# Transposing small tiles on VectorE instead of TensorE, and a new order for short matrix products in a hybrid attention trunk

## The chip, the cores and the metric

The kernel runs on one core of a Trainium2 chip. The metric is device time in microseconds for one execution of the whole program. One execution was also recorded by the hardware profiler. All stretches, rows and waits below come from that record.

The engines have short names in the profile: PE is TensorE (matrix products), PEld its loads of the stationary operand, DVE is VectorE, ACT is ScalarE, POOL is GpSimd, and SP issues most DMAs. L180 means line 180 of the kernel before.

## What is computed

The reference is a two-layer trunk over 512 tokens of width 1024, with 16 learned "meta" tokens prepended. Each layer normalises the residual, projects it, runs two causal mixers side by side (a pooling mixer and a latent attention with 8 heads) and adds the gated sum back. Cut to what matters here:

```python
kv = (c_kv @ w_kv_b).reshape(B, L, N_HEADS, QK_NOPE_DIM + V_HEAD_DIM)
k_nope, v = kv[..., :QK_NOPE_DIM], kv[..., QK_NOPE_DIM:]
...
q = rmsnorm(q, g_qn)
k = rmsnorm(k, g_kn)
...
s = jnp.einsum('bqhd,bkhd->bhqk', q[:, q0:kend], k[:, :kend]).astype(jnp.float32) * scale
s = jnp.where(valid, s, MASK_VALUE)
p = jax.nn.softmax(s, axis=-1).astype(v.dtype)
outs.append(jnp.einsum('bhqk,bkhd->bqhd', p, v[:, :kend]))
...
h_res = h_res + merged @ w_out[l]
```

Every ordinary token attends to the 16 meta tokens and to the ordinary tokens before it. Each meta token attends to the meta tokens before it. The meta tokens' own outputs are needed after layer 0 but not after layer 1.

## The kernel before

**Precision by splitting.** Each float32 operand is split into a high part in the fast matrix format (`fp32r`) and the low rest. ScalarE makes the high part by a copy, VectorE the low part by a subtraction. The helper `split` does this for a tile. A product then takes three passes, high x high, high x low and low x high (`mm3`, L180 to L182).

**Stream and order.** All projections of both layers form one list (`plan`), run by the generator `stream` in steps of a few passes. The layer's other work is written by hand in `Layer.go` and pulls the stream forward with `step`, `fill`, `fill_now` and `upto`, so that projection passes stand between the parts of the attention. `after` defers a piece by an amount of stream time; `LAG` is 2000 ns. The written order is a priority: a scheduler then places every instruction on its engine's queue by a simulated time line, taking the first in the written order whose operands are ready there. `behind(a, b)` makes `a` wait for `b`.

**Attention.** `head` handles one head: score products into PSUM tiles named S, masking and row extremum on VectorE (`top`), exponentials on ScalarE (`expo`), normalisation on POOL (L818 for the 16 meta columns, L820 for the rest). Query tile i holds 128 queries, and its keys are the meta tokens and the 128(i+1) tokens up to its end. The score product of query tile 0 has 144 columns.

The probabilities of the head before (`prev`) are multiplied with the values in `pv`. For every key tile j, TensorE transposes the 4-j probability tiles (L839), `split` takes them out of PSUM as `th` and `tl`, and two products add to the output tile `o`: one with a stationary of 128 columns (high and low values side by side, L844), and one with a stationary of 64 columns (L845) for the low probabilities. `pv(prev, (0, 1))` does key tiles 0 and 1, `pv(prev, (2, 3))` the other two. `go` calls the second one after the next head's `prep`.

**Meta tokens.** The 16 meta columns of the probabilities of two heads are collected in `pm`, 128 x 4 x 32 numbers. At the odd head, `pv` splits `pm` into `pmr` (L833, L834), transposes it by four products with an identity (`identr`, L850), and copies the result out of PSUM into `mt`, as high, low and high again (L853, L854). One product of `mt` with the block-diagonal meta values `vb` then adds the meta part for both heads (L868). `vb` is made in `v_body`: six passes of 512 columns with the meta tokens' latent replicated eight times as stationary (tile name `pa`), then a mask and copies that move rows between partitions (L673 to L675).

**Small sums.** The squared norms of queries and keys are summed by products into two PSUM tiles, copied to SBUF by `stat_rows`, transposed in `qk_stats` by five TensorE transposes (L716, L717) and turned into factors by Newton steps on VectorE. In `meta_queries` (layer 0), the meta tokens' own probabilities are transposed by one TensorE transpose (L889) and spread by small copies.

Of the kernel before, what the change touches and what calls it, by code (L numbers as in the profile page):

```python
# [71 lines left out]
def trunk(ctx, tc, xT, xrow, mrow, pos, win, wkr, wqb, wkb, wvb, wgr, wpu, wmu, wout, gains, const, yT):  # L72
# [65 lines left out]
    gp.memset(maskw[:, :512 - P], 0.0)  # L138
    identr = cp.tile([P, P], F32R, name="identr")

    def other_loads(made):
        for k in range(2, 8):
            behind(sp.dma_start(xb[:, k, :T], xT[:, k, :]), made)
            if k in (3, 4):
                raw = rawt()
                behind(sp.dma_start(raw, win[0, MT_CKV + k - 3, :, 512:1024]), made)
                early.append(raw)
        behind(sp.dma_start(cst, const), made)
        behind(sp.dma_start(posb[:, :T], pos.partition_broadcast(P)), made)
        dve.tensor_copy(maskw[:, 512 - P:], cst[:, C_MASK:C_MASK + P])  # L150
        dve.tensor_copy(identr, ident)

# [117 lines left out]
    def split(hi, lo, src, a, b):  # L270
        act.activation(hi[:, a:b], src, AF.Copy)  # L271
        dve.tensor_sub(lo[:, a:b], src, hi[:, a:b].bitcast(F32))  # L272

# [35 lines left out]
    class Layer:  # L309
# [191 lines left out]

        def stat_rows(self, x0):
            t = tmp()
            for s, (a, b) in enumerate(FULL):
                a = max(a, x0)
                g, o_ = 32 * s, HALF * s
                act.activation(t[0:H, a:b], self.st[s][g:g + H, a - o_:b - o_], AF.Copy)
                dve.tensor_add(t[0:H, a:b], self.st[s][g + 64:g + 64 + H, a - o_:b - o_], t[0:H, a:b])
            return t

        def k_sums(self):
            self.stat_go(5)
            sp.dma_start(ksr[self.l], self.stat_rows(0)[0:H, 0:T])

# [122 lines left out]
        def v_body(self, k, w):  # L637
# [18 lines left out]
            for k in range(2):  # L656
                rep = []
                for t in cs[k]:
                    r = slot("pa", F32R, bufs=2, w=416)[:, 0:P].rearrange("p (a b) -> p a b", a=8)
                    dve.tensor_copy(r, t[:, 0:NM].bitcast(F32).unsqueeze(1).to_broadcast([P, 8, NM]))  # L660
# [3 lines left out]
            dve.scalar_tensor_tensor(out=vf[:, :512].rearrange("p (a b) -> p a b", a=8),  # L664
                                     in0=ps.rearrange("p (a b) -> p a b", a=8), scalar=self.ninv[:, 4:5],
                                     in1=cst[:, C_VBD:C_VBD + 8].unsqueeze(2).to_broadcast([P, 8, 64]),
                                     op0=ALU.mult, op1=ALU.mult)
            fh, fl = tmp(), tmp()
            act.activation(fh[:, :512].bitcast(F32R), vf[:, :512], AF.Copy)
            dve.tensor_sub(fl[:, :512].bitcast(F32R), vf[:, :512], fh[:, :512])  # L670
            for p in range(4):
                r, c = slice(32 * p, 32 * p + 32), slice(P * p, P * p + P)
                gp.tensor_copy(self.vb[0:32, c], fh[r, c])  # L673
                act.activation(self.vb[32:64, c], fh[r, c], AF.Copy)
                gp.tensor_copy(self.vb[64:96, c], fl[r, c])  # L675
            yield 6 * 216
# [30 lines left out]
        def qk_stats(self):  # L707
            fill_now(LAG + 100)
            self.stat_go(7)
            sts = self.stat_rows(self.x0)  # L710
            if self.last:
                dve.memset(sts[0:H, 0:NM], 1.0)
            fill_now(2600)
            stp = mmt()
            for j in range(4):
                pe.transpose(stp[:, H * j:H * j + H], sts[0:H, NM + P * j:NM + P * (j + 1)], ident[0:H, 0:H])  # L716
            pe.transpose(stp[0:NM, 4 * H:5 * H], sts[0:H, 0:NM], ident[0:H, 0:H])  # L717
            na, ny, nt = (sm.tile([P, 5, H], F32, tag=t, name=nm(t)) for t in ("na", "ny", "nt"))
            dve.memset(na[:, 4, :], 1.0)
            eps = self.eps.unsqueeze(2).to_broadcast([P, 5, H])  # L720
            for r, j, k in ((P, 0, 4), (NM, 4, 5)):
                dve.scalar_tensor_tensor(out=na[0:r, j:k, :], in0=stp[0:r, H * j:H * k].rearrange("p (a b) -> p a b", b=H),
                                         scalar=1.0 / QK, in1=eps[0:r, j:k, :], op0=ALU.mult, op1=ALU.add)
            newton(ny, na, nt)
            self.nqs = sm.tile([P, 5, H], F32, tag="nqs", name=nm("nqs"))
            dve.tensor_scalar(self.nqs, ny, -1.0 / math.sqrt(QK), None, op0=ALU.mult)
            fill_now(9500)
            if not self.last:
                self.smeta = sm.tile([NM, 8, NM], F32, tag="smeta", name=nm("smeta"))

# [28 lines left out]
        def head(self, h, kq, prev):  # L759
# [62 lines left out]

        def pv(self, prev, js):
            if prev is None:
                return
            h, pt, pm = prev
            p, odd = h // 2, h % 2
            if js[0] == 0:
                self.o = sct() if h == H - 1 else pp.tile([P, 512], F32, tag="o", name=nm("o"), bufs=1)
            ops = self.o  # L830
            if odd == 1 and js[0] == 0:
                self.pmr = sm.tile([P, 4, 2, 32], F32R, tag="pmr", name=nm("pmr"))
                act.activation(self.pmr[:, :, 0, :], pm, AF.Copy)  # L833
                dve.tensor_sub(self.pmr[:, :, 1, :], pm, self.pmr[:, :, 0, :].bitcast(F32))  # L834
            for j in js:
                n = SEQ - P * j
                tr = mmt()
                for i in range(j, 4):
                    pe.transpose(tr[:, P * (i - j):P * (i - j + 1)], pt[i][:, NM + P * j:NM + P * (j + 1)], ident)  # L839
                th = tp.tile([P, W], F32R, tag="th", name=nm("th"), bufs=2)  # L840
                tl = tp.tile([P, W], F32R, tag="tl", name=nm("tl"), bufs=2)
                split(th, tl, tr[:, :n], 0, n)
                out = ops[:, P * j:512]
                pe.matmul(out, vt[:, j, h, :], th[:, :n], start=j == 0, stop=j == 3)  # L844
                pe.matmul(out[0:64], vt[:, j, h, 0:64], tl[:, :n], start=False, stop=j == 3, skip_group_check=True)  # L845
            if js[-1] != 3:
                if odd == 1:
                    tr = sct() if h == H - 1 else mmt()
                    for i in range(4):
                        pe.matmul(tr[0:64, P * i:P * (i + 1)], self.pmr[:, i].rearrange("p a b -> p (a b)"), identr,  # L850
                                  start=True, stop=True)
                    self.mt = slot("racc", F32R)
                    act.activation(self.mt[0:64, 0:512], tr[0:64, :], AF.Copy)  # L853
                    act.activation(self.mt[64:96, 0:512], tr[0:32, :], AF.Copy)  # L854
                return
            if odd == 0:
                self.op = tmp()
# [19 lines left out]
        def meta_queries(self):  # L877
# [9 lines left out]
            dve.tensor_mul(smeta, smeta, bc(mxm))  # L887
            tr = mmt()
            pe.transpose(tr[:, 0:NM], smeta.rearrange("p a b -> p (a b)"), ident[0:NM, 0:NM])  # L889
            mh = sm.tile([96, 4 * NM], F32R, tag="mh", name=nm("mh"))  # L890
            for p in range(4):
                r, c = slice(32 * p, 32 * p + 32), slice(NM * p, NM * p + NM)
                act.activation(mh[0:32, c], tr[r, 0:NM], AF.Copy)
                act.activation(mh[64:96, c], tr[r, 0:NM], AF.Copy)
                dve.tensor_sub(mh[32:64, c], tr[r, 0:NM], mh[0:32, c].bitcast(F32))
            self.mo = sm.tile([P, 4 * NM], F32, tag="mo", name=nm("mo"))
# [120 lines left out]
        def go(self, nxt):  # L1017
# [52 lines left out]
            self.pv(prev, (0, 1))  # L1070
            if not self.last:
                self.meta_queries()
            fill_now(2600)
            self.pv(prev, (2, 3))
            up("gm7")
# [86 lines left out]
```

## Time and profile before

| | |
|---|---|
| time, median of 3 runs | 778.08 us (778.04 to 778.8) |
| time of the profiled execution | 778.45 us |
| its span, first to last instruction | 776.6 us |
| instructions in the span | 14527 |
| granted TensorE clock, mean | 0.999 |

A row of the profile's groups names the line, engine and operation, what is written and read, the shapes, the count, and then the busy time in us and the mean ns of one. Timelines give start and duration in us. A matrix product's duration overlaps the next one's, since TensorE pipelines them; the distance between starts shows the pace. Some records of matrix products are missing from the trace, so counts of neighbours in a timeline can be one short.

### The profile page before, as it was taken

The numbers are of one execution on the slowest core, as the hardware profiler recorded it, in microseconds if no ns is written. First come the engines' busy times: TensorE is split into PE (matmuls) and PEld (weight loads), VectorE is DVE, ScalarE is ACT, GpSimd is POOL, SyncE is SP. The second block draws the span as 40 slices with busy tenths as digits, with TensorE's granted clock in tenths as the row PEclk, the third lists the DMA queues.
The fourth block names the chain that finished last, engine by engine and source line by source line (L and its number), as shares of the span: only waits on it lengthen the run. The fifth ranks groups of instructions, "written<-read, shape, count | busy, mean of one in ns | idle before, by whom it ended". The sixth has DMA issues, their size and how long they took to land.

```text
span 776.6 us, 14527 instructions
## 1 busy us (share of the span) xinstructions
PE 771.7 (99%) x5251; PEld 702.8 (90%) x5251; DVE 534.3 (69%) x1155; ACT 414.2 (53%) x930; POOL 206.9 (27%) x265
## 2 busy tenths in 40 slices
PE   9999999999999999999999999999999999999998
PEld 8999899999999999999997898887788888888887
DVE  5588688357788977785466486774577888765932
ACT  6755656545666665633354365455446666654420
POOL 1026404012334242052120263030132433420500
PEclk9999999999999999999999999999999999999999
DMA  8533234433222222325643332244232332122372
GB/s 284 164 112 98 74 92 123 123 96 103 92 82 87 79 67 71 96 82 153 188 134 91 110 89 87 79 132 141 76 123 89 96 89 89 59 79 68 108 241 85
DMA packets 54932, 84.04 MB, mean 108 GB/s; under 512 B 10007, under 2 KB 18583, under 8 KB 54861
## 3 DMA queue, kind: packets, MB, share of 16 engines
q1 hardware_dynamic: 54716, 82.86, 35.2%
q8 instruction: 41, 0.67, 0.4%
q14 instruction: 31, 0.25, 0.1%
q10 hardware_dynamic: 144, 0.26, 0.1%
HBM read 76.68 MB, written 4.29 MB: 104 GB/s over the span
## 4 chain that ended last, share of the span: by engine, by line
PE 99%; DMA 1%; SPq 0%; ACT 0%; DVE 0%; issue 0%
PE mm L180 29%; PE mm L182 29%; PE mm L181 29%; PE mm L839 2%; PE S L181 2%; PE S L182 2%; PE S L180 2%; PE o L844 1%; PE o L845 1%; PE S L498 1%; DMA raw<-win 1%; PE S L462 0%; PE mm L868 0%; PE mm L387 0%; PE mm L850 0%; PE S L845 0%
## 5 line engine op out<-in xcount | busy, mean ns | idle before, releaser
L180 PE MATMUL mm<-hh,whi 128*128 128x264 f32 (+2 forms) x1096 | 345.4, 317 | 0.3 <-ACT whi L175 0.3
L181 PE MATMUL mm<-hl,whi 128*128 128x264 f32 (+2 forms) x1096 | 343.2, 314 | 0.0
L182 PE MATMUL mm<-hh,wlo 128*128 128x264 f32 (+2 forms) x1096 | 342.5, 314 | 0.0
L176 DVE TENSOR_TENSOR wlo<-raw,whi 128x512 fp32r<-128x512 f32 (+2 forms) x251 | 181.4, 726 | 103.7 <-ACT whi L175 101.4
L175 ACT ACTIVATE whi<-raw 128x512 fp32r<-128x512 f32 (+2 forms) x251 | 150.5, 603 | 178.9 <-PE mm L181 134.3
L180 PEld LDWEIGHTS mm<-hh,whi 128*128 128x128 f32 x1096 | 205.5, 188 | 13.6 <-ACT whi L175 0.5
L181 PEld LDWEIGHTS mm<-hl,whi 128*128 128x128 f32 x1096 | 206.1, 188 | 12.0
L182 PEld LDWEIGHTS mm<-hh,wlo 128*128 128x128 f32 x1096 | 205.2, 188 | 12.2
L743 POOL TENSOR_TENSOR tmp<-kp,bc 64x528 f32<-64x528 f32 x16 | 24.8, 1552 | 103.7 <-issue 53.5
L818 POOL TENSOR_TENSOR pm<-pa,rs 128x16 f32<-128x16 f32 x32 | 11.7, 365 | 148.6 <-DVE rs L813 148.6
L604 POOL TENSOR_TENSOR racc<-racc,tmp 128x264 f32<-128x264 f32 (+1 forms) x15 | 14.3, 957 | 113.9 <-ACT tmp L603 113.9
L928 POOL TENSOR_TENSOR tmp<-tmp,xb 128x264 f32<-128x264 f32 (+1 forms) x24 | 26.7, 1134 | 57.7 <-DVE tmp L926 55.5
L774 DVE CUSTOM_DVE_ANT_0 S<-S,maskw,nqs 128x272 f32<-128x272 f32 (+4 forms) x80 | 38.4, 498 | 2.2 <-PE S L182 1.9
L180 PE MATMUL mm<-u,whi 128*128 128x264 f32 (+1 forms) x108 | 35.1, 325 | 0.0
L182 PE MATMUL mm<-u,wlo 128*128 128x264 f32 (+1 forms) x108 | 34.7, 321 | 0.0
L180 PE MATMUL mm<-cq,whi 128*128 128x264 f32 (+1 forms) x108 | 34.6, 321 | 0.0
L181 PE MATMUL mm<-cq,whi 128*128 128x264 f32 (+1 forms) x108 | 34.6, 321 | 0.0
L182 PE MATMUL mm<-cq,wlo 128*128 128x264 f32 (+1 forms) x108 | 34.6, 320 | 0.0
L272 DVE TENSOR_TENSOR tl<-mm,th 128x512 fp32r<-128x512 f32 (+1 forms) x64 | 29.3, 482 | 7.0 <-ACT th L271 6.0
L781 ACT ACTIVATE cq<-S,bia 128x400 f32<-128x400 f32 (+2 forms) x48 | 24.5, 515 | 17.8 <-DVE bia L808 8.8
L820 POOL TENSOR_TENSOR cq<-cq,rs 128x384 f32<-128x384 f32 (+1 forms) x32 | 33.5, 1047 | 0.0
L271 ACT ACTIVATE th<-mm 128x512 fp32r<-128x512 f32 (+1 forms) x64 | 25.4, 434 | 6.5 <-PE mm L839 5.9
(271 smaller groups left out, 1370.8 us busy)
## 6 DMA issues: line engine op xcount, KB each, us to landing
raw<-win SPq DMA_DIRECT2D x143, 256.0 KB, 2.6
raw<-wout SPq DMA_DIRECT2D x32, 256.0 KB, 3.0
bc<-kdr SPq DMA_DIRECT2D x16, 264.0 KB, 3.1
raw<-wpu SPq DMA_DIRECT2D x16, 256.0 KB, 2.9
raw<-wmu SPq DMA_DIRECT2D x16, 256.0 KB, 2.7
raw<-wqb SPq DMA_DIRECT2D x12, 256.0 KB, 3.0
xb<-xT SPq DMA_DIRECT2D x8, 264.0 KB, 5.5
tmp<-xT SPq DMA_DIRECT2D x16, 132.0 KB, 3.4
```

The source lines that it names most:

```text
L175: act.activation(hi[:, :n], raw[:, :n], AF.Copy)
L176: dve.tensor_sub(lo[:, :n], raw[:, :n], hi[:, :n].bitcast(F32))
L180: pe.matmul(out, wh, xh, start=start, stop=False)
L181: pe.matmul(out, wh, xl, start=False, stop=False)
L182: newest[0] = pe.matmul(out, wl, xh, start=False, stop=stop)
L271: act.activation(hi[:, a:b], src, AF.Copy)
L272: dve.tensor_sub(lo[:, a:b], src, hi[:, a:b].bitcast(F32))
L743: gp.tensor_mul(kf[r0:r0 + 64, :], self.kp[r0:r0 + 64, :], bc[r0:r0 + 64, :])]
L774: dve.tensor_tensor_reduce(out=sv, in0=sv, in1=mask, scale=nqs[:, i, h:h + 1], scalar=3e38, op0=ALU.add, op1=ALU.min, accum_out=bia[:, c:c ...
L781: act.activation(pv, sv, AF.Exp, scale=-1.0, bias=bia[:, i:i + 1], accum_out=rs[:, c:c + 1])
L820: gp.tensor_mul(pt[i][:, NM:], pt[i][:, NM:], rs[:, i:i + 1].to_broadcast([P, n - NM]))
L928: gp.tensor_add(t[:, :b - a], t[:, :b - a], self.am[m][:, a:b])
```

## The change

Six things change together.

1. The meta probabilities `pm` are transposed by VectorE, in blocks of 32 x 32, into `turn`. This is then split, and the blocks are put in place by four small ScalarE copies, four small VectorE copies and one larger ScalarE copy. The four identity products, their PSUM tile and `identr` go.
2. The small sums of `qk_stats` are transposed by VectorE from a zeroed tile `srows`. Scaling and adding epsilon become five small scalings and one addition. The one transpose of `meta_queries` also moves to VectorE.
3. The meta values take four passes instead of six: stationaries of 64 columns (two copies each of the high and the low latent) and of 32 columns. The two row groups of the result are added, masked, and written to `vb` by three instructions. Eight POOL copies go.
4. `pv` now has three parts. Part 0 transposes and splits key tiles 0 and 1, each into its own tile. Part 1 makes their products (for the last head of a layer in part 0). Part 2 transposes key tiles 2 and 3 into one PSUM tile, splits them together and makes their products in the order high 2, high 3, low 3, low 2.
5. In layer 0, from the second head on, the three 144-column score passes of query tile 0 are placed between the products of part 1, and the low product of key tile 0 is cut in two. In layer 1, part 1 stands right behind part 0, and the score passes stay.
6. `follow` keeps the written order among such passes, and `ready` lets one of them wait for the split of the low part.

The diff, with context and small renamings cut:

```diff
-    identr = cp.tile([P, P], F32R, name="identr")
+    srows = cp.tile([32, T], F32, name="srows")
+    gp.memset(srows, 0.0)
...
-        dve.tensor_copy(identr, ident)
...
+    def follow(ins, other):
+        tc.add_manual_dep(ins.ins, other.ins.name,
+                          mybir.DependencyInfo(mybir.DependencyClass.NoSync, mybir.DependencyReason.SCHED_ONLY))
...
             for k in range(2):
-                rep = []
-                for t in cs[k]:
-                    r = slot("pa", F32R, bufs=2, w=416)[:, 0:P].rearrange("p (a b) -> p a b", a=8)
-                    dve.tensor_copy(r, t[:, 0:NM].bitcast(F32).unsqueeze(1).to_broadcast([P, 8, NM]))
-                    rep.append(r.rearrange("p a b -> p (a b)"))
-                mm3(ps, rep[0], rep[1], wv[k][0], wv[k][1], k == 0, k == 1)
-            vf = tmp()
-            dve.scalar_tensor_tensor(out=vf[:, :512].rearrange("p (a b) -> p a b", a=8),
...
-            for p in range(4):
-                r, c = slice(32 * p, 32 * p + 32), slice(P * p, P * p + P)
-                gp.tensor_copy(self.vb[0:32, c], fh[r, c])
-                act.activation(self.vb[32:64, c], fh[r, c], AF.Copy)
-                gp.tensor_copy(self.vb[64:96, c], fl[r, c])
+                r = slot("pa", F32R, bufs=2, w=416)[:, 0:4 * NM].rearrange("p (a b) -> p a b", a=4)
+                for i, t in enumerate(cs[k]):
+                    dve.tensor_copy(r[:, 2 * i:2 * i + 2, :],
+                                    t[:, 0:NM].bitcast(F32).unsqueeze(1).to_broadcast([P, 2, NM]))
+                r = r.rearrange("p a b -> p (a b)")
+                pe.matmul(ps[0:64], r, wv[k][0], start=k == 0, stop=k == 1)
+                newest[0] = pe.matmul(ps[0:32], r[:, 0:32], wv[k][1], start=False, stop=k == 1, skip_group_check=True)
+            vf, t = tmp(), tmp()
+            act.activation(t[0:32, :512], ps[32:64, :], AF.Copy)
+            dve.tensor_add(t[0:32, :512], ps[0:32, :], t[0:32, :512])
+            for e in range(2):
+                v4 = [x[0:32, :512].rearrange("p (a e b) -> p a e b", a=4, e=2)[:, :, e, :] for x in (vf, t)]
+                dve.tensor_scalar(v4[0], v4[1], self.ninv[0:32, 4:5], cst[0:32, C_VBD + e:C_VBD + e + 1],
+                                  op0=ALU.mult, op1=ALU.mult)
+            act.activation(self.vb[0:32, :], vf[0:32, :512], AF.Copy)
+            dve.tensor_sub(self.vb[64:96, :], vf[0:32, :512], self.vb[0:32, :].bitcast(F32))
+            act.activation(self.vb[32:64, :], vf[0:32, :512], AF.Copy)
...
-            stp = mmt()
-            for j in range(4):
-                pe.transpose(stp[:, H * j:H * j + H], sts[0:H, NM + P * j:NM + P * (j + 1)], ident[0:H, 0:H])
-            pe.transpose(stp[0:NM, 4 * H:5 * H], sts[0:H, 0:NM], ident[0:H, 0:H])
+            stp = tmp(WU)
+            dve.transpose(stp[0:32, 0:512], sts[0:32, NM:T])
+            dve.transpose(stp[0:32, 512:544], sts[0:32, 0:32])
...
+            for c in range(4):
+                dve.tensor_scalar(na[32 * c:32 * c + 32, 0:4, :], v[:, :, c, 0:H], 1.0 / QK, None, op0=ALU.mult)
+            dve.tensor_scalar(na[0:NM, 4, :], stp[0:NM, 512:512 + H], 1.0 / QK, None, op0=ALU.mult)
+            dve.tensor_add(na, na, self.eps.unsqueeze(2).to_broadcast([P, 5, H]))
...
-            self.pv(prev, (0, 1))
+            self.pv(prev, 0)
+            if self.last:
+                self.pv(prev, 1)
             self.gap()
...
             scores(3, s4, SPL, T)
-            scores(0, s0, 0, 144)
+            if prev is None or self.last:
+                scores(0, s0, 0, 144)
+            else:
+                q0 = slice(NM, NM + P)
+                self.pv(prev, 1, [lambda k=k, q=q, x=x: pe.matmul(s0, q[:, q0], x[:, 0:144], start=k == 0, stop=k == 2)
+                                  for k, (q, x) in enumerate(((qh, kh), (qh, kl), (ql, kh)))])
...
+                if odd == 1:
+                    turn = sm.tile([P, P], F32, tag="pmt", name=nm("pmt"))
+                    ph, pl = (sm.tile([P, P], F32R, tag=t, name=nm(t)) for t in ("pmh", "pml"))
+                    dve.transpose(turn, pm.rearrange("p a b -> p (a b)"))
+                    split(ph, pl, turn, 0, P)
+                    self.mt = slot("racc", F32R)
+                    for c in range(4):
+                        r = slice(32 * c, 32 * c + 32)
+                        v = lambda t: t.rearrange("p (a b) -> p a b", a=4)
+                        d = lambda g: v(self.mt[g:g + 32, 0:512])[:, :, r]
+                        act.activation(d(0), v(ph[r, :]), AF.Copy)
+                        dve.tensor_copy(d(32), v(pl[r, :]).bitcast(F32))
+                    act.activation(self.mt[64:96, 0:512], self.mt[0:32, 0:512], AF.Copy)
...
+            def both(j, t, c):
+                n = SEQ - P * j
+                return pe.matmul(ops[:, P * j:512], vt[:, j, h, :], t[0][:, c:c + n], start=j == 0, stop=j == 3)
+
+            def low(j, t, c, a=0, b=512):
+                a, b = max(a, P * j), min(b, 512)
+                return pe.matmul(ops[0:64, a:b], vt[:, j, h, 0:64], t[1][:, c + a - P * j:c + b - P * j],
+                                 start=False, stop=j == 3, skip_group_check=True)
...
+            if part == 0:
+                self.t01 = [turned((0,)), turned((1,))]
+            if part == (0 if final else 1):
+                t0, t1 = self.t01
+                if hosts:
+                    chain(lambda: both(0, t0, 0), lambda: ready(t0, hosts[0]), lambda: low(0, t0, 0, 0, 256), hosts[1],
+                          lambda: low(0, t0, 0, 256, 512))
+                    chain(lambda: both(1, t1, 0), lambda: ready(t1, hosts[2]), lambda: low(1, t1, 0))
+                else:
+                    for j, t in enumerate(self.t01):
+                        both(j, t, 0)
+                        low(j, t, 0)
+            if part < 2:
                 return
+            t = turned((2, 3))
+            chain(lambda: both(2, t, 0), lambda: ready(t, lambda: both(3, t, 256)), lambda: low(3, t, 256), lambda: low(2, t, 0))
...
-            tr = mmt()
-            pe.transpose(tr[:, 0:NM], smeta.rearrange("p a b -> p (a b)"), ident[0:NM, 0:NM])
+            tr = sm.tile([32, P], F32, tag="smt", name=nm("smt"))
+            dve.transpose(tr, self.smeta32.rearrange("p a b -> p (a b)"))
...
-                self.pv(prev, (2, 3))
+                self.pv(prev, 2)
```

More of the change, by code (lines that the diff above doesn't have):

```diff
@@ L827, in pv @@
             p, odd = h // 2, h % 2
-            if js[0] == 0:
-                self.o = sct() if h == H - 1 else pp.tile([P, 512], F32, tag="o", name=nm("o"), bufs=1)
-            ops = self.o
[L831 to L836, printed above, removed]
-                tr = mmt()
-                for i in range(j, 4):
-                    pe.transpose(tr[:, P * (i - j):P * (i - j + 1)], pt[i][:, NM + P * j:NM + P * (j + 1)], ident)
+            final = h == H - 1
@@ L840, in pv, with turned @@
+            ops = self.o
+            def turned(js):
+                tr, c = mmt(), 0
+                for j in js:
+                    for i in range(j, 4):
+                        pe.transpose(tr[:, c:c + P], pt[i][:, NM + P * j:NM + P * (j + 1)], ident)
+                        c += P
                 th = tp.tile([P, W], F32R, tag="th", name=nm("th"), bufs=2)
                 tl = tp.tile([P, W], F32R, tag="tl", name=nm("tl"), bufs=2)
-                split(th, tl, tr[:, :n], 0, n)
-                out = ops[:, P * j:512]
@@ L844, in pv @@
[L844 to L854, printed above, removed]
+                return th, tl, split(th, tl, tr[:, :c], 0, c)
@@ new lines, in ready @@
+            def ready(t, fn):
+                ins = fn()
+                behind(ins, t[2])
+                return ins
+            def both(j, t, c):
[5 more added lines that the diff above has]
+                                 start=False, stop=j == 3, skip_group_check=True)
@@ new lines, in chain @@
+            def chain(*fns):
+                last = None
+                for fn in fns:
+                    ins = fn()
+                    if last is not None:
+                        follow(ins, last)
+                    last = ins
+            if part == 0:
+                self.t01 = [turned((0,)), turned((1,))]
[9 more added lines that the diff above has]
+                        low(j, t, 0)
```

42 lines of the change are left out of this document (17 added, 25 removed).

## The prediction, made before the changed kernel was built or run

> **What bounds the kernel now.** I read the page first, then the waits of TensorE, then its timeline at the places the change touches, and last the rows of VectorE.
>
> ```profile
> PE 771.7 (99%) x5251; PEld 702.8 (90%) x5251; DVE 534.3 (69%) x1155; ACT 414.2 (53%) x930; POOL 206.9 (27%) x265
> ...
> PE 99%; DMA 1%; SPq 0%; ACT 0%; DVE 0%; issue 0%
> ```
> ```profile
> core 0 of [0], span 776.6 us
> engine line waited for: us in total, times, longest us
> PE wps L136 <- DVE na L719: 1.1, 1, 1.1
> PE S L180 <- ACT hh L332: 0.5, 1, 0.5
> PE mm L180 <- ACT whi L175: 0.3, 1, 0.3
> ```
>
> The first fence is the page's busy line and its chain of work that ended last: TensorE 99% on both. The second is everything TensorE waited for: 1.9 us of 776.6, all at the start. The instruction stream of TensorE itself is the time, so every nanosecond taken out of that stream shortens the kernel as long as nothing then fails to keep up. A busy row is too coarse for this, because matmuls overlap (a pass of 264 columns lasts 0.28 us and the next one starts after 0.12). The measure I use is the distance between starts in TensorE's timeline, whose columns are start and duration in us, line, operation, shapes.
>
> **The change part by part, TensorE first.** The product of the meta tokens' values with the weights (`v_body`, stationary copies named pa):
>
> ```profile
> 480.21 0.39 PE L180 MATMUL mm<-whi,pa 128*128 128x512 f32 x1
> 480.44 0.39 PE L181 MATMUL mm<-wlo,pa 128*128 128x512 f32 x1
> ```
>
> A pass of 512 columns takes 0.23 us between starts. There are six per layer, and four after the change (two stationaries of 64 and two of 32 columns): 2 x 2 layers x 0.23 = **0.92 us** less. The streamed columns set the time of a pass, so narrower stationaries gain nothing further.
>
> The transposes of the small sums (`qk_stats`, L716 and L717, eight rows in, five per layer):
>
> ```profile
> 153.28 0.28 PE L182 MATMUL mm<-u,wlo 128*128 128x264 f32 x1
> 153.49 0.22 PE L716 MATMUL mm<-cst,tmp 8*128 8x8 f32 x1
> 153.64 0.39 PE L180 MATMUL mm<-u,whi 128*128 128x264 f32 x1
> 153.87 0.29 PE L181 MATMUL mm<-th,whi 128*128 128x264 f32 x1
> ...
> 155.09 0.28 PE L182 MATMUL mm<-u,wlo 128*128 128x264 f32 x1
> 155.30 0.35 PE L716 MATMUL mm<-cst,tmp 8*128 8x8 f32 x3
> 155.51 0.16 PE L717 MATMUL mm<-cst,tmp 8*16 8x8 f32 x1
> 155.60 0.39 PE L180 MATMUL mm<-u,whi 128*128 128x264 f32 x1
> 155.83 0.28 PE L181 MATMUL mm<-th,whi 128*128 128x264 f32 x1
> 155.95 0.28 PE L182 MATMUL mm<-u,wlo 128*128 128x264 f32 x1
> ```
>
> Two passes of 264 columns need 2 x 0.12. From 153.28 to 153.87 they need 0.59, so the lone transpose costs 0.35; from 155.09 to 155.83 it is 0.74, so the other group costs 0.50. The cost is not the eight columns but going into and out of that shape. I take layer 1 as layer 0: 2 x 0.85 = **1.70 us** less. The one transpose of the meta queries (`meta_queries`, layer 0 only, 16 rows) has no cheaper neighbour than the lone one: **0.35 us**.
>
> The transposes of the meta probabilities (`pv`, L850, four per pair of heads, eight pairs):
>
> ```profile
> 282.29 0.40 PE L850 MATMUL mm<-identr,pmr 128*64 128x128 f32 x4
> 282.52 0.34 PE L180 MATMUL S<-kh,qhl 128*128 128x272 f32 x1
> 282.70 0.28 PE L181 MATMUL S<-kl,qhl 128*128 128x272 f32 x1
> ...
> 316.51 0.40 PE L850 MATMUL S<-identr,pmr 128*64 128x128 f32 x4
> ```
>
> From 282.29 to 282.70 is 0.41, and 0.12 of it is the score pass: 0.29 for the group, 0.23 for its columns and 0.06 because the next full stationary cannot be loaded behind so short a pass. 8 x 0.29 = **2.32 us** less. (The last row is the next pair's group, 34 us on.)
>
> The score passes that move (three of 144 columns per head):
>
> ```profile
> 229.96 0.23 PE L180 MATMUL S<-kh,qhl 128*128 128x144 f32 x1
> 230.03 0.27 PE L181 MATMUL S<-kl,qhl 128*128 128x144 f32 x1
> 230.14 0.28 PE L182 MATMUL S<-kh,qhl 128*128 128x144 f32 x1
> 230.25 0.33 PE L180 MATMUL mm<-hh,whi 128*128 128x264 f32 x1
> 230.41 0.29 PE L181 MATMUL mm<-hl,whi 128*128 128x264 f32 x1
> ```
>
> The first is followed after 0.07, its columns' time; from 229.96 to 230.41 they and one pass of 264 columns need 0.45 instead of 3 x 0.07 + 0.12 = 0.33. A 144-column pass is too short to cover the load of a 128-column stationary. The change puts each ahead of a product with a stationary of 64 columns (`low`), and behind a long one. All 0.12 to 0.13 should go, in layer 0 for heads 1 to 7 (head 0 has no predecessor, layer 1 keeps the old order): 7 x 0.13 = **0.91 us**. One `low` becomes two of 256 columns, the same columns.
>
> The end of each head's probability products (L844, L845):
>
> ```profile
> 258.74 0.22 PE L844 MATMUL o<-th,vt 128*128 128x128 f32 x1
> 258.80 0.22 PE L845 MATMUL o<-tl,vt 128*64 128x128 f32 x1
> 258.86 0.34 PE L180 MATMUL mm<-hh,whi 128*128 128x264 f32 x1
> 259.04 0.29 PE L181 MATMUL mm<-hl,whi 128*128 128x264 f32 x1
> ```
>
> The 128-column `low` is last, and the pass after it takes 0.18 instead of 0.12. After the change the 256-column `low` is last and covers the load: 16 heads x 0.06 = 0.96, of which I take **0.90 us**. The ten transposes of probabilities per head stay as they are.
>
> Sum: 0.92 + 1.70 + 0.35 + 2.32 + 0.91 + 0.90 = **7.1 us** less on TensorE.
>
> **What the other engines get for it.**
>
> ```profile
> L834 DVE TENSOR_TENSOR pmr<-pm,pmr x8: 286/770/774, 203.5 to 694.3; 128x128 fp32r<-128x128 f32 x8
> ```
> ```profile
> L660 DVE CAST pa<-kh x4: 203/210/218, 18.1 to 477.6; 128x128 fp32r<-128x128 f32 x4
> ```
> ```profile
> L674 ACT ACTIVATE vb<-tmp 32x128 fp32r<-32x128 f32 x8 | 2.5, 309 | 0.1
> ```
> ```profile
> 255.00:275.00 20.00, 20.00 (x164) 19.78 (x162) 18.83 (x48) 13.26 (x37) 8.18 (x15) 1.00 0.26 74
> ```
> ```profile
> ACT pmr L833 <- POOL pm L818: 12.3, 7, 2.7
> ```
>
> These are durations by tile or line (min/median/max or mean ns), a stretch of 20 us (busy us of PE, PEld, DVE, ACT, POOL) and a wait (us, times, longest). Per pair of heads VectorE gets one transpose of 128 x 128, which no row shows: between 0.21 (a copy of that size) and 0.77 (the subtraction of the same pm tile, 0.29 at best). I take 0.3, nearer the copy, as it too has one input. It also gets four copies of 32 x 128, at most 0.21 each by the copy's row, 0.84 together; its subtraction stays. ScalarE gets four copies of 0.31 and loses one of two evacuations. Splitting the third and fourth probability tiles together saves each engine one instruction per head. That is roughly 1.1 us more on VectorE per pair, nine in all, against 776.6 - 534.3 = 242 us in which it idles. I put it at nothing: a pair of heads lasts 34 us, and even the densest stretch leaves VectorE 20.00 - 18.83 = 1.17 us. If that cover is gone it costs what the last rival says. The transpose waits for POOL's pm where ScalarE waits now (12.3 us in seven waits); behind it on VectorE queue weight splits and the next head's row maxima. What they release is weights and probabilities, and TensorE has projection passes to run meanwhile. In `qk_stats` the two transposes and the small scalings, each like the 0.2 us instructions around them, replace a trip through TensorE. In `v_body` eight POOL copies go; `vb` is first read a whole head pair later. The two memsets on POOL stand far ahead of their readers, and no DMA is added or moved past another.
>
> The sum is made on the profiled execution, 778.45 us for a span of 776.6; it stands 0.37 above the median of 778.08. 778.45 - 7.1 = 771.3, and against the median **771.0 us**.
>
> **Two rules weighed.** L834 alone takes 0.29 us and mostly 0.77, with POOL's normalising beside it. The Trainium skill (SBUF — State Buffer, "SBUF: two separate sides") says that VectorE and GpSimd share a port pair as an exclusive lock, taken by a VectorE instruction with two SBUF inputs or in a two-port mode, and that the loser blocks. That fits, and speaks against adding VectorE copies just there; by it each added copy may block a POOL step or be blocked by one, which changes nothing while both have idle time. The eight-row transposes pay on entry and exit. The Trainium skill (TensorEngine Tiling (Array Packing), "Key Properties") says that changing the tiling mode drains TensorE; the 64-column `low` at 258.80 is entered and left without such a gap, so by the trace a narrow stationary alone does not.
>
> **The rivals.**
> *The narrow value products drain.* The stationaries of 32 columns may be a mode of their own, entered four times. Priced as the lone transpose: 4 x 0.35 = 1.4, so 772.4 us. For it: L716. Against: the 64-column rows. 8%.
> *The order gains fail.* If other projection passes are slipped between the moved passes, their long loads return: 0.91 + 0.90 lost, 772.8 us. For it: in the present timeline such passes do stand between score passes and products. Against: the added order edges and priority. 12%.
> *TensorE's gaps are handed to waits.* If weights arrived no faster than they are used now, the freed time would turn into waiting: 778 us. For it: TensorE never waits today, so spare supply is not seen there directly. Against: VectorE and ScalarE idle 31% and 47%. 8%.
> *VectorE sets the pace in the attention stretches: slower.* Per pair at worst a transpose of 0.77, copies of 0.84 and the longest wait of 2.7 move onto VectorE: 4.3 us. Less the 1.17 idle of the densest stretch it is 3.1 us behind. If TensorE paid that in every pair, 8 x 3.1 = 25 us less the 7.1: 796 us; it decides from the third pair on (7.1 / 3.1 = 2.3), while one bad pair leaves 774.1. For it: 18.83 of 20. Against: on the page VectorE idles 31%, and weights are split ahead of need. 12%.
>
> **How the numbers follow.** The forecast itself, 770 to 772.2, has 60%. The range reaches on to the two small rivals and one bad pair of the last, with a little below for groups of L850 that cost more than the one priced: 769.8 to 775.5. A measurement here tells 0.2% (1.6 us) from no change. Faster: 60 + 8 + 12, with a one-pair share of the last rival, 2: 82%. Same: 8%. Slower: 10%.
>
> **What would show it.** Right: TensorE 99% busy and waiting under 3 us, no L716, L850 or L889 instructions, four pa products per layer, 144-column passes 0.07 apart from a 64-column successor, no short `low` ahead of a projection pass, VectorE near 540 us. The forecast is wrong if TensorE's waits grow by several microseconds on weights (whi, wlo) or on th and tl, or if gaps of 0.3 stand around the 32-column passes.

## The result, and the profile after

| | before | after |
|---|---|---|
| median | 778.21 us (4 runs, 778.04 to 778.8) | 773.7 us (4 runs, 773.59 to 773.9) |
| profiled execution / its span | 778.45 / 776.6 us | 773.65 / 771.8 us |

The ratio is 0.9936, 95% interval 0.9925 to 0.9948: faster by 4.5 us, where 7.1 were forecast. The page's busy line and its chain after the change, then all that TensorE waited for (us in total, times, longest):

```profile
PE 765.3 (99%) x5211; PEld 697.6 (90%) x5211; DVE 542.9 (70%) x1192; ACT 417.8 (54%) x928; POOL 199.5 (26%) x251
...
PE 98%; DVE 1%; DMA 0%; ACT 0%; issue 0%; SPq 0%; DVEq 0%; ACTq 0%
```
```profile
PE S L181 <- ACT cq L785: 1.1, 1, 1.1
PE wps L136 <- DVE na L720: 1.1, 1, 1.1
PE mm L181 <- DVE tmp L975: 0.9, 1, 0.9
PE S L181 <- ACT hh L337: 0.2, 1, 0.2
```

The first and third wait are new. By starts of matmuls (distance to the next start, less the pace of its columns), they cost 1.27 us at 279 us, in layer 0's attention, and 1.10 us at 339 us, in the meta update: 2.37 us. From the first to the last start of a matmul the time fell by 4.77 us, so the stream became 7.14 us shorter.

The removed transposes are on VectorE now. The first row below is from the groups, the second from the view of one line (min/median/max ns), the rest from TensorE's timeline:

```profile
L717 DVE STREAM_TRANSPOSE tmp<-srows 32x512 f32<-32x512 f32 x2 | 1.4, 679 | 0.0
```
```profile
L845 DVE STREAM_TRANSPOSE pmt<-pm x8: 295/306/311, 203.3 to 689.2; 128x128 f32<-128x128 f32 x8
```
```profile
475.25 0.40 PE L667 MATMUL mm<-wlo,pa 128*32 128x512 f32 x1
475.49 0.40 PE L666 MATMUL mm<-whi,pa 128*64 128x512 f32 x1
475.73 0.40 PE L667 MATMUL mm<-wlo,pa 128*32 128x512 f32 x1
...
230.96 0.23 PE L815 MATMUL S<-kh,qhl 128*128 128x144 f32 x1
231.03 0.28 PE L878 MATMUL o<-tl,vt 128*64 128x256 f32 x1
231.15 0.23 PE L815 MATMUL S<-kl,qhl 128*128 128x144 f32 x1
231.21 0.28 PE L878 MATMUL o<-tl,vt 128*64 128x256 f32 x1
231.33 0.34 PE L874 MATMUL o<-th,vt 128*128 128x384 f32 x1
```

The 32-column passes keep the pace of their columns (0.24 us, no gap), and each 144-column pass is followed after 0.06 to 0.07 us.

**The first new wait.** VectorE's timeline before the wait, after and before the change (start, us, engine, line; in brackets its idle time and what ended it):

```profile
273.36 0.31 DVE L845 STREAM_TRANSPOSE pmt<-pm 128x128 f32<-128x128 f32 x1 [1.07 <-POOL pm L829]
274.05 0.42 DVE L273 TENSOR_TENSOR pml<-pmt,pmh 128x128 fp32r<-128x128 f32 x1 [0.38 <-ACT pmh L272]
274.50 1.74 DVE L746 TENSOR_TENSOR tmp<-kn,bc 64x528 f32<-64x528 f32 x1
276.27 0.68 DVE L853 CAST racc<-pml 32x128 fp32r<-32x128 f32 x3
276.98 0.51 DVE L778 CUSTOM_DVE_ANT_0 S<-S,maskw,nqs 128x272 f32<-128x272 f32 x1
...
278.56 0.45 DVE L778 CUSTOM_DVE_ANT_0 S<-S,maskw,nqs 128x240 f32<-128x240 f32 x1
```
```profile
274.48 0.50 DVE L774 CUSTOM_DVE_ANT_0 S<-S,maskw,nqs 128x272 f32<-128x272 f32 x1
...
275.08 0.48 DVE L774 CUSTOM_DVE_ANT_0 S<-S,maskw,nqs 128x240 f32<-128x240 f32 x1
...
275.80 0.77 DVE L834 TENSOR_TENSOR pmr<-pm,pmr 128x128 fp32r<-128x128 f32 x1 [0.19 <-ACT pmr L833]
276.58 1.75 DVE L742 TENSOR_TENSOR tmp<-kn,bc 64x528 f32<-64x528 f32 x1
```

Before, two of the head's row extrema (272 and 240 columns) stand in front of the meta step, which waits 0.19 us. After, the meta step is in front. VectorE stands idle for 1.07 us until POOL has normalised the fourth slice of `pm` and for 0.38 us until ScalarE has rounded it. It then spends 1.74 us on the key factors and 0.68 on three of the new copies, and the extrema come last.

That looks like the cause, but the tile that TensorE waits for hangs on the third extremum, of 400 columns, and that one stands behind the meta step and the key factors in both kernels. Its rows, then the exponential that reads the tile, then TensorE's last pass before the wait and the pass that waited, after the change; and below, the first two before it:

```profile
278.95 0.63 DVE L778 CUSTOM_DVE_ANT_0 S<-S,maskw,nqs 128x400 f32<-128x400 f32 x1
279.67 0.60 ACT L785 ACTIVATE cq<-S,bia 128x400 f32<-128x400 f32 x1
279.00 0.29 PE L183 MATMUL S<-kh,qhl 128*128 128x288 f32 x1
280.40 0.39 PE L181 MATMUL S<-kh,qhl 128*128 128x272 f32 x1 [1.11 <-ACT cq L785]
```
```profile
279.16 0.64 DVE L774 CUSTOM_DVE_ANT_0 S<-S,maskw,nqs 128x400 f32<-128x400 f32 x1
279.90 0.59 ACT L781 ACTIVATE cq<-S,bia 128x400 f32<-128x400 f32 x1 [0.30 <-DVE bia L774]
```

Count from the head's first score pass, which starts at 272.66 us after the change and at 273.13 before it. The tile is back after 7.60 us now and was back after 7.37 us, so it comes 0.23 us later. But TensorE asks for it, for the next head's scores, at 6.47 us now (280.40 less the stall), and asked at 9.39 us before (282.52, the row of 272 columns in the prediction): 2.92 us earlier. (It is the same tile in both: of the three S tiles, the first holds the scores of 240 columns, which are read at 285.69 us before and 286.83 after, and the third has just been filled.) The kernel before had 2.0 us to spare, and the changed one is 1.1 us short. Most of this wait comes from TensorE's own new order, in which 30 projection passes stand between the two heads' scores where 48 stood before; VectorE's delay adds 0.23 us.

**The second new wait** lies in code that the diff doesn't touch. From the timeline after the change:

```profile
338.50 0.98 DVE L273 TENSOR_TENSOR hl<-tmp,hh 128x264 fp32r<-128x264 f32 x1
...
339.41 0.68 DVE L177 TENSOR_TENSOR wlo<-raw,whi 128x512 fp32r<-128x512 f32 x1
340.01 0.41 DVE L975 SCALAR_TENSOR_TENSOR tmp<-cq,mm 128x264 f32<-128x264 f32 x1
...
340.57 0.36 PE L181 MATMUL mm<-q,whi 128*128 128x264 f32 x1 [0.94 <-DVE tmp L975]
```

VectorE runs from one instruction to the next; L975, which empties the PSUM tile that TensorE needs, stands behind a weight split. The window around it (busy us of PE, PEld, DVE, ACT, POOL) has VectorE at 12.22 of 13 us:

```profile
331.00:344.00 13.00, 12.06 (x99) 11.86 (x98) 12.22 (x22) 6.34 (x14) 8.45 (x10) 1.00 0.27 82
```

### The profile page after: what moved, and what is told of

Same layout as the page of the kernel before. It is cut to its first block, busy times and chain, and to the rows that moved or that the text cites. A ratio compares the mean times of both kernels' runs of the same rounds, so it can differ in the third digit from the quotient of the medians.

```text
span 771.8 us, 14407 instructions
## 1 busy us (share of the span) xinstructions
PE 765.3 (99%) x5211; PEld 697.6 (90%) x5211; DVE 542.9 (70%) x1192; ACT 417.8 (54%) x928; POOL 199.5 (26%) x251
## 4 chain that ended last, share of the span: by engine, by line
PE 98%; DVE 1%; DMA 0%; ACT 0%; issue 0%; SPq 0%; DVEq 0%; ACTq 0%
PE mm L181 29%; PE mm L183 29%; PE mm L182 29%; PE mm L861 2%; PE S L181 2%; PE S L182 2%; PE S L183 2%; PE o L874 1%; PE o L878 1%; PE S L503 1%; PE S L467 0%; DVE wlo L177 0%; DMA xb<-xT 0%; DVE hl L273 0%; PE mm L917 0%; PE mm L392 0%
## 5 line engine op out<-in xcount | busy, mean ns | idle before, releaser
L778 DVE CUSTOM_DVE_ANT_0 S<-S,maskw,nqs 128x400 f32<-128x400 f32 (+4 forms) x80 | 38.4, 496 | 5.0 <-PE S L815 2.8
L273 DVE TENSOR_TENSOR tl<-mm,th 128x384 fp32r<-128x384 f32 (+1 forms) x48 | 28.0, 592 | 5.8 <-ACT th L272 5.6
L272 ACT ACTIVATE th<-mm 128x384 fp32r<-128x384 f32 (+1 forms) x48 | 24.2, 523 | 9.5 <-PE mm L861 9.2
```

Of the source, the lines that this page charges most:

```text
L273: return dve.tensor_sub(lo[:, a:b], src, hi[:, a:b].bitcast(F32))
L778: dve.tensor_tensor_reduce(out=sv, in0=sv, in1=mask, scale=nqs[:, i, h:h + 1], scalar=3e38, op0=ALU.add, op1=ALU.min, accum_out=bia[:, c:c ...
```

## The experiments

"Stalls" are gaps of at least 0.2 us between starts on TensorE beyond the columns' pace, after the first 30 us. The profiled executions of `p_v` and `u_pm` lie 1.6 to 1.8 us above their medians, so their times are taken from the medians alone.

**One part alone.** `p_pm`: the kernel before with the meta probabilities transposed on VectorE.

```diff
-  split pm into pmr; four products with identr; two ScalarE copies
+  dve.transpose(turn, pm.rearrange("p a b -> p (a b)")); split(ph, pl, turn, 0, P)
+  per 32 rows: act.activation(d(0), ...); dve.tensor_copy(d(32), ...)
```

> The kernel before with one part of the change: the meta probabilities are transposed by VectorE (L850 gone). Theory A, the time is TensorE's stream plus its stalls: 8 groups of 0.29 to 0.31 us leave the stream, 2.3 to 2.5 us, so 775.7 us if TensorE waits no more than its 1.9 us of before; with the small VectorE copies as the cause of the stall at 279 us in the changed kernel, a similar stall of 0.5 to 1.5 us shows in an attention pair and the time is 776.3 to 777.2. Rival B, the stalls come from any change of the planned order and not from these copies: no stall tied to a VectorE chain, 775.7.

779.52 us, ratio 1.0011 [1.0001, 1.002]. The 32 products are gone, and without its stalls the stream is 2.0 us shorter (2.32 were forecast). But stalls of 0.67, 1.29, 0.41 and 0.36 us stand at 237 to 268 us, and one of 0.29 at 57 us. Before the 1.29 at 245 us VectorE stands idle for 1.97 us in front of the transpose, one pair earlier than above; TensorE then waits for an instruction further down VectorE's queue (L793):

```profile
243.25 0.31 DVE L832 STREAM_TRANSPOSE pmt<-pm 128x128 f32<-128x128 f32 x1 [1.97 <-POOL pm L816]
246.56 0.41 PE L846 MATMUL mm<-cst,pa 128*128 128x128 f32 x2 [1.13 <-DVE smeta L793]
```

`p_stats`: the kernel before with the small sums and the meta queries transposed on VectorE.

```diff
-  pe.transpose(stp[...], sts[...], ident[0:H, 0:H])   # five, and one in meta_queries
+  dve.transpose(stp[0:32, 0:512], sts[0:32, NM:T]); dve.transpose(stp[0:32, 512:544], sts[0:32, 0:32])
```

> The kernel before with the small sums and the meta queries' probabilities transposed by VectorE. Theory A: 2 x 0.85 + 0.35 = 2.05 us leave TensorE's stream, 776.1 us, and TensorE's waits stay near 1.9 us. Rival (VectorE's longer chain makes TensorE wait for the factors of the first head): 777 or more, with a wait near 155 or 548 us.

776.63 us, ratio 0.9971 [0.9961, 0.9981]: 1.8 us less than the 778.44 beside it, where its terms say 2.05. One stall, of 0.34 us at 57 us, accounts for the difference; there is none in the attention.

`p_v`: the kernel before with four value products instead of six.

```diff
-  mm3(ps, rep[0], rep[1], wv[k][0], wv[k][1], k == 0, k == 1)
+  pe.matmul(ps[0:64], r, wv[k][0], ...); pe.matmul(ps[0:32], r[:, 0:32], wv[k][1], ...)
```

> The kernel before with the meta values in four products. Theory A: four passes of 0.23 us less, 0.92 us, 777.2 us. Rival (stationaries of 32 columns are entered and left with a drain of 0.35 us, four times): 778.6 us, and gaps of 0.1 to 0.2 us on both sides of the 32-column passes in the timeline.

777.93 us, ratio 0.9992 [0.9982, 1.0002]: 0.5 less, where its term says 0.92. The interval doesn't part it from no change.

`p_order`: the kernel before with the three parts of `pv` and the score passes between products; the meta probabilities stay on TensorE.

```diff
-  self.pv(prev, (0, 1)); ...; scores(0, s0, 0, 144); ...; self.pv(prev, (2, 3))
+  self.pv(prev, 0); ...; self.pv(prev, 1, [three 144-column passes]); ...; self.pv(prev, 2)
```

> The kernel before with the new order of the probability products and score passes alone; the three transposes stay on TensorE and the meta values in six products. Theory A: 7 x 0.13 + 16 x 0.055 = 1.8 us less, 776.3 us. Rival (other projection passes slip between and their long loads return): 778.1 us, with 144-column passes still followed after 0.11 us.

779.74 us, ratio 1.0016 [1.0007, 1.0026]. VectorE has no copy more than before, and yet stalls of 0.20, 0.84, 0.25, 0.35 and 1.01 us stand at 257 to 283 us, and one of 0.23 at 323 us. The last of the five is the change's first wait. On VectorE the meta step is again in front, here in its old form, and yet the tile is back no later than in the kernel before, 7.34 us after the head's first score pass at 276.43 us; TensorE asks for it at 6.47 us:

```profile
278.28 0.77 DVE L849 TENSOR_TENSOR pmr<-pm,pmr 128x128 fp32r<-128x128 f32 x1 [1.41 <-ACT pmr L848]
283.18 0.59 ACT L789 ACTIVATE cq<-S,bia 128x400 f32<-128x400 f32 x1
283.91 0.39 PE L183 MATMUL S<-kh,qhl 128*128 128x272 f32 x1 [0.85 <-ACT cq L789]
```

The four parts alone make +1.1, -1.8, -0.5 and +1.3 us, together nothing, while the whole change makes -4.5: the stalls don't add.

**One part undone.** `u_pm`: the changed kernel with the meta probabilities on TensorE again.

```diff
-  dve.transpose(turn, ...); split(ph, pl, turn, 0, P); nine small copies
+  split pm into pmr; pe.matmul(tr[0:64, P * i:P * (i + 1)], pmr[:, i], identr); two ScalarE copies
```

> The changed kernel with the meta probabilities transposed by TensorE as before. Theory A: 2.4 us come back into TensorE's stream and the stall at 279 us goes (-1.3): 774.8 us. Rival B, stalls are accidents of the plan: 2.4 us more stream and 0 to 3 us of other stalls in the attention of layer 0, 775 to 779.

777.14 us, ratio 0.998 [0.9969, 0.9991], 3.4 above the change. The stalls come at the same offsets as in `p_order` (0.20, 0.87, 0.24, 0.35, 1.00) and that in the meta update is gone, so they are only 0.3 more than the change has; some 3 us is what the 32 products cost TensorE, more than the 2.32 forecast.

`u_hosts`: the changed kernel with the 144-column passes in a row again.

```diff
-            if prev is None or self.last:
+            if True:
                 scores(0, s0, 0, 144)
+                if prev is not None and not self.last:
+                    self.pv(prev, 1)
```

> The changed kernel with the three 144-column score passes of layer 0 in a row again, ahead of the products of part 1. Theory A: 7 x 0.13 = 0.9 us come back into the stream, 774.6 us if the two stalls stay as they are. Rival: the passes were not hosted in effect and nothing changes, 773.7.

777.08 us, ratio 0.9983 [0.9974, 0.9993], 3.4 above. Gaps of 0.06 to 0.15 us on TensorE grow by about 1.0 us in sum, which is the term of 0.91. The rest is mostly stalls: 4.0 us at 242 to 283 us and none in the meta update, where the change has 2.4 in all.

**Load or order.** `c_pool`: the changed kernel with the four new VectorE copies on POOL.

```diff
-                        dve.tensor_copy(d(32), v(pl[r, :]).bitcast(F32))
+                        gp.tensor_copy(d(32), v(pl[r, :]).bitcast(F32))
```

> The changed kernel with the four small copies of the low meta probabilities on POOL instead of VectorE (L853). Theory A, the stall of 1.27 us at 279 us comes from VectorE, where these four copies of 0.22 us stand between a lengthened product with the key factors and the next head's row extremum: the stall goes or falls under 0.4 us, 772.4 to 772.8 us, while the stall of 1.1 us in the mu stage stays. Rival B, every edit re-plans the order and the stalls are the plan's accidents: this one may go, but others of 0.5 to 3 us in all turn up in the attention of layer 0, 773 to 776 us.

774.37 us, ratio 0.9941 [0.9926, 0.9956]. In place of the stall at 279 us there are three, of 0.37, 0.54 and 0.37 us at 262, 264 and 280 us: 1.28 in sum as against 1.27. The stall in the meta update stays. Taking the copies from VectorE gained nothing.

`c_prep`: the changed kernel with the VectorE half of the key factors on POOL in layer 0.

```diff
-            made = [dve.tensor_mul(kf[n0:n0 + 64, :], ...
+            made = [(dve if self.last else gp).tensor_mul(kf[n0:n0 + 64, :], ...
```

> The changed kernel with the VectorE half of the key-factor product (L746) on GpSimd in layer 0's stage, which takes 0.9 to 1.7 us of VectorE's time per head away. Theory A (VectorE was late at the row extremum before 279 us because it was full): the wait of 1.3 us at 279 us goes and the time is 772.4 us. Rival (a re-planned stretch gets new waits elsewhere, or GpSimd is now late with the key factors): stalls of 1 us or more in 155 to 320 us, 773.5 us or above. On the stage behind (339 us) theory A says nothing changes: 1.1 us there.

776.45 us, ratio 0.997 [0.9959, 0.9981]: the rival. Stalls of 1.00, 0.85, 0.23, 0.35 and 0.93 us stand at 255 to 282 us, and the one in the meta update stays at 1.10. VectorE's wait for `pm` stays at 1.07 us a time (its waits from 237 to 285 us, where the change has one of 1.1: us, times, longest):

```profile
DVE pmt L845 <- POOL pm L829: 2.1, 2, 1.1
```

`c_less`: the changed kernel with two pieces of VectorE work left out, as its expectation says.

```diff
+            if self.last or h < 2:
                 dve.tensor_sub(ql[n0:n0 + 64, x0:T], src, ...)
```

> The changed kernel without the low parts of the meta update's second half in layer 0, and besides without the low parts of the queries of layer 0's heads 2 to 7 (L757 left out there; old low parts stand in their place). This takes 0.7 us per head from VectorE and gives it to no other engine; no product on TensorE goes. Theory A (the wait of 1.3 us at 279 us is VectorE being full, and the price of the change is nothing but such waits): no stall is left and the time is what TensorE's stream alone makes of the forecast, 771.2 us. Rival B (in a stretch that is planned anew waits remain wherever the planned order misses, whatever VectorE's load is): stalls of 0.4 to 3 us in 237 to 283 us, 771.8 to 774.5 us.

773.35 us, ratio 0.9933 [0.9916, 0.995]: the rival. Stalls of 0.28, 0.49 and 0.60 us at 247 and 280 us, and one of 0.21 at 207 us, though VectorE was given 0.7 us per head. Part of the work left out became waiting in front of the same step (again 237 to 285 us):

```profile
DVE pmt L846 <- POOL pm L830: 2.2, 2, 1.2
```

The wait at 279 us shrinks, since the tile is back after 6.97 us instead of 7.60, but it stays: VectorE's load bears on its size but does not make it. Two windows say the same: VectorE is busier in `p_stats`, which has no stall over 237 to 285 us, than in the change, which has one. Here are the sums, in that order:

```profile
sum 48.00, PE 48.00 PEld 47.35 DVE 43.16 ACT 31.06 POOL 17.19; mean PE 24.00 PEld 23.68 DVE 21.58 ACT 15.53 POOL 8.59
```
```profile
sum 48.00, PE 46.89 PEld 46.23 DVE 42.60 ACT 31.45 POOL 17.01; mean PE 23.44 PEld 23.12 DVE 21.30 ACT 15.73 POOL 8.51
```

What parts the kernels is when TensorE asks. For this pair of heads (273 to 287 us) the table has, in us from the head's first score pass, when the exponential of 400 columns ends and so hands the tile back, when TensorE reaches the next head's scores, and TensorE's stall at that point:

| run | tile back | asked for | stall |
|---|---|---|---|
| before | 7.37 | 9.39 | none |
| `p_stats` | 7.36 | 9.38 | none |
| `p_v` | 7.35 | 9.39 | none |
| `p_pm` | 8.76 | 9.2 | none |
| `n_fill` | 10.98 | 13.6 | none |
| change, `c_muless` | 7.60 | 6.47 | 1.27 |
| `c_mu` | 7.59 | 6.47 | 1.27 |
| `u_hosts` | 8.02 | 6.47 | 1.69 |
| `p_order` | 7.34 | 6.47 | 1.01 |
| `u_pm` | 7.33 | 6.47 | 1.00 |
| `c_less` | 6.97 | 6.50 | 0.60 |

In the seven kernels with this stall, it is each time the lateness of the tile plus about 0.14 us. In `n_fill` and `p_pm` the tile comes back latest of all, and no stall follows, because TensorE asks later still. (`c_pool` and `c_prep` ask 18.7 and 19.3 us after the head's first score pass, and have no stall at that point either.) The seven have the three-part `pv` in common. `p_order` shows that the transposes on VectorE aren't needed for it, and `u_hosts` that the moved score passes aren't. But `c_pool` and `c_prep` have that `pv` too, so it is the plan as a whole that puts the scores early or late. This is read from the traces; no run forced one order of TensorE on another plan.

**The stall in the meta update.** `c_mu`: the changed kernel in which one more product of layer 0's meta update goes to tiles of the S kind.

```diff
-                if (l, m) == (0, 2):
+                if l == 0 and m in (2, 4):
```

> The changed kernel with one more pair of PSUM tiles for the products of the mu stage of layer 0 (the fifth product takes two of the idle S tiles). Theory A, at 339 us TensorE waits for a PSUM tile whose evacuation (L975) stands behind a weight split on VectorE: with two more tiles the wait of 1.1 us goes, 772.6 us, and nothing else moves. Rival (it waits for weights, not for the tile): 773.7.

773.72 us, ratio 0.9933 [0.9918, 0.9948]. The wait moves to 345.5 us and keeps its size, so more tiles only put it off:

```profile
PE mm L181 <- DVE tmp L975: 1.0, 1, 1.0
```

`c_muless`: the changed kernel without eight subtractions there.

```diff
+                if not self.last and a > 0:
+                    act.activation(self.mg[m][0][:, a:b], t[:, :b - a], AF.Copy)
+                    return
                 split(*self.mg[m], t[:, :b - a], a, b)
```

> The changed kernel without the low parts of the meta update's result for the second half of the tokens in layer 0 (the rounding to the high part stays, the subtraction that makes the low part is left out, so the output lacks those low parts). It takes eight subtractions of about 0.7 us from VectorE in the stage at 332 to 357 us. Theory A (the 1.1 us wait at 339 us is VectorE running behind in that stage): that wait goes, 772.6 us. Rival (it is a tile handed back in a bad order, whatever VectorE has to do): it stays at 0.8 us or more, 773.5 us.

772.41 us, ratio 0.9921 [0.9907, 0.9936]. That stall is gone and nothing else moved. All that TensorE waits for after its first 30 us:

```profile
PE S L181 <- ACT cq L785: 1.1, 1, 1.1
```

In this stage, unlike the other, it is VectorE running behind. Why it does so here and not in the kernel before, whose code for this stage is the same, stays open.

**A new plan and nothing else.** `n_fill`: the kernel before with one number of its plan changed.

```diff
-FILL = (2950.0, 2850.0)
+FILL = (3000.0, 2850.0)
```

> The kernel before with one number of the planner changed, FILL[0] from 2950 to 3000: no instruction is added or removed, only the order on the engines may come out otherwise. Theory A (the stalls seen in layer 0's attention between 237 and 283 us come from the added VectorE work): no stalls of TensorE after its first 30 us, 778.2 us. Theory B (any new plan of a stretch in which VectorE is about 95 % busy can make them, since the plan is made from estimated costs): stalls of 0.5 to 3 us there, 778.7 to 781 us.

781.51 us, ratio 1.0037 [1.0023, 1.0051]: 3.0 us slower with the same instructions. The longest of TensorE's new waits:

```profile
PE mm L180 <- DVE tmp L926: 1.2, 1, 1.2
```

By starts all of them come to 3.0 us: 1.7 at 269 to 322 us, and 1.34 at 344 us, on the same evacuation as the change's second wait (L926 is its line in the kernel before). So the kernel before stood at a good plan, and a loss of 1 to 3 us needs no added work.

## Why the prediction was right, and where it missed

The sum over TensorE's stream was right: 7.1 forecast, 7.14 found. Single terms are less sure than their sum: the small sums gave 2.1 for 2.05 once their one stall is taken out, the value products 0.5 for 0.92, and the meta transposes 2.0 for 2.32 when made alone but some 3 when undone. Of the rivals, the narrow products do not drain (0.24 us per pass), the order gains do not fail (0.06 to 0.07 us), and no wait on weights appears.

The time missed the forecast all the same: 773.7 us lies above the 770 to 772.2 that the forecast itself had, and inside the whole range by luck, as that reached on to rivals that did not come about as they were described.

The step that missed is the price of new waits, "I put it at nothing"; they cost 2.37 us. The cover that it named, VectorE's idle time, does not decide whether TensorE waits. The prediction did name the transpose's wait for `pm` and that the row maxima queue behind it, and then let TensorE run projection passes meanwhile, as if its order stayed as it was. At one pair the new order put the next head's scores ahead of such passes: TensorE asked 2.92 us earlier for a tile that came back 0.23 us later. The wait it priced, 12.3 us in seven, was ScalarE's. VectorE's own idle time at this step over the whole run (us, times), for the subtraction before and the transpose after, is:

```profile
  ACT pmr L833: 6.7, 7
```
```profile
  POOL pm L829: 3.9, 4
```

The subtraction behind the transpose waits another 1.6 us in four for its rounding, so VectorE's new waits at this step, 5.5 us, are not longer than the old one.

The rival in which VectorE sets the pace had the mechanism's place, and its case of one bad pair (774.1 us) lies close to 773.7, by luck. Its working, a sum of added durations against idle time, isn't what happened: the time falls neither when the copies are moved (`c_pool`) nor, by more than 0.4 us, when other VectorE work is left out (`c_less`). And of the 2.37 us lost, 1.10 is in a stage that the change doesn't touch. The prediction had no term for work that is merely planned anew; `n_fill` shows that this alone is worth 3 us here.

What the change is worth therefore depends on the plan it meets. With the parts taken singly, stalls of about 3 us each turned two of them into losses; together they cost 2.4 once.

## What to carry to other kernels

Where one engine's stream is the time, count that stream start to start: the sum comes out. Then ask, for every tile that the stream takes again, when the new order asks for it and when it is handed back; the busy share of the engine that hands it back answers neither. And where a scheduler orders the queues from estimated times, run the old kernel once with a harmless change of plan: its spread (here 3 us) is what a single part must beat before its time says anything about the part.

## What the runs showed of the hardware

The key-factor product on 64 x 528 numbers (min/median/max ns in the change, 155 to 320 us):

```profile
L746 DVE TENSOR_TENSOR tmp<-kn,bc x8: 689/704/1744, 167.2 to 274.5; 64x528 f32<-64x528 f32 x8
```

It takes 0.69 us alone and 1.74 with POOL's half of it running beside (274.28 to 275.67 us). At 167 us VectorE starts first (167.18, POOL at 167.28): VectorE takes 0.70 us, and POOL's product 1.80 where it takes 1.34 alone (170.94). The kernel before has the same 1.75 us on VectorE at this pair, without a stall, so the change did not bring it. That the later one loses agrees with the Trainium skill (SBUF — State Buffer, "SBUF: two separate sides"), by which a VectorE instruction with two inputs in SBUF and GpSimd exclude each other on a shared port. The measurements add that VectorE's instruction lost 1.04 us to a POOL instruction of 1.39 us.
